# Code placement, SyncE drains and a reshaped last quarter in a fused row-dot and softmax kernel

## The chip, the cores and the metric

One core of a Trainium2 chip. The metric is the device time of one execution in microseconds (us); lower is better. Each run also has its *span*, the time between the first and the last recorded instruction. The timed figure is about 2 us longer than the span.

## The reference

```python
# x, y: 8 x 4096 x 512 fp32
gram = np.matmul(x, y.transpose(0, 2, 1))
diag = np.diagonal(gram, axis1=1, axis2=2)      # 8 x 4096: one dot of 512 per row
diag = diag - diag.max(axis=-1, keepdims=True)
exp = np.exp(diag)
return exp / exp.sum(axis=-1, keepdims=True)
```

Only the diagonal is needed: 32,768 dots of 512 elements, then eight softmaxes of 4096. Both inputs, 134.22 MB, must be read once.

## The kernel before

Four batches lie on 128 partitions (32 partitions each), so two halves of four steps make S = 8 steps. One step is 32 rows for each partition. Helpers used below: `products` is one wide multiply on VectorE, in place in x; `sums` is one reduction on VectorE; `sums_act` is one ScalarE copy per row with an accumulator; `dots` is one fused multiply-and-sum per row on VectorE; `largest` is a maximum over columns on VectorE. K = 6: `side` is ScalarE's copy of the last six rows of y, so that y's only buffer comes free before they are multiplied. The columns of `diag` beyond C = 128 hold maxima.

```python
xs = [big.tile([P, R, D], f32, name=f"xs{i}") for i in range(2)]   # R = 32, D = 512
ys = big.tile([P, R, D], f32, name="ys")                           # one buffer only
diag = [small.tile([P, C + 2 * i], f32, name=f"diag{i}") for i in range(B // Q)]  # C = 128
# ... helpers cut ...
for t in range(S - 2):                       # steps 0 to 5
    load_x(t, 0, R)
    load_y(t, 0, R)
    nc.scalar.activation(out=side, in_=ys[:, R - K :, :], func=Act.Copy)
    products(t, 0, R - K, ys[:, : R - K, :])
    # ... (finish half 0 during step 4) ...
    products(t, R - K, K, side)
    sums(t, 0, R - W)
    sums_act(t, R - W, W)                    # W = 2 rows on ScalarE
    # ... (maximum and exponential of half 0 at the end of step 3) ...

t = S - 2                                    # step 6
load_x(t, 0, R)
for r0 in (0, H):                            # H = 16
    load_y(t, r0, H)
    dots(t, r0, H)

t += 1                                       # step 7, in ever smaller pieces
r0 = 0
for n in (16, 8, 4, 2, 1, 1):
    load_x(t, r0, n)
    load_y(t, r0, n)
    if r0 == 0:
        largest(diag[1][:, C : C + 1], diag[1][:, : C - R])
    if r0 == R - 2:
        largest(diag[1][:, C + 1 :], diag[1][:, C - R : C - 2])
    dots(t, r0, n)
    r0 += n

for p in range(0, P, G):                     # store half 0
    nc.sync.dma_start(out=ov[0, p : p + G, :], in_=res[0][p : p + G, :])
normalize(1, exps(1, diag[1][:, C - 2 :]))   # max, exp, sum, scale
nc.scalar.dma_start(out=ov[1], in_=res[1])   # store half 1
```

## Time and profile before

| | before |
|---|---|
| timed, median of 3 (range) | 321.22 us (321.2 to 321.28) |
| span of the profiled run (timed 321.27) | 319.15 us |
| first load issued / first packet / last load landed | 0.73 / 1.76 / 314.15 us |
| VectorE busy | 76% |

In the profile's timeline a line gives start, duration, engine, line of the program and operation, `output<-input`, and in brackets the idle time before it with what ended it. "SPq" and "ACTq" are DMA issues. The trace also records each DMA packet and each of the 16 increments by which a load tells that its 16 parts have landed (512 increments for the 27 loads and 5 stores of the kernel before). "Spread" below is the time from a load's first increment to its last. Here are the start and the end of the timeline of the kernel before:

```profile
0.73 1.28 ACT L116 ACT_TABLE_LOAD   x1 [0.73 <-PEq L162]
0.73 0.39 SPq L63 DMA_DIRECT2D xs<-in_x_dram  x1
...
312.97 0.18 DVE L97 TENSOR_REDUCE diag<-diag 128x1 f32<-128x30 f32 x1
313.08 0.68 DVE L83 SCALAR_TENSOR_TENSOR xs<-xs,ys 128x512 f32<-128x512 f32 x1
...
314.24 0.69 DVE L83 SCALAR_TENSOR_TENSOR xs<-xs,ys 128x512 f32<-128x512 f32 x1 [0.48 <-DMA ys<-in_y_dram]
...
315.17 0.21 DVE L91 TRANSPOSE_TENSOR_REDUCE nmx<-mxp 128x1 f32<-128x32 f32 x1
315.48 0.40 ACT L104 ACTIVATE res<-diag,nmx 128x128 f32<-128x128 f32 x1 [61.06 <-DVE nmx L91]
...
316.77 0.37 ACTq L147 DMA_DIRECT2D out_dram<-res  x1
```

The reader should see that the very last dot waits for data (0.48 us), and that what follows it is a short serial chain: maximum over partitions (`nmx`), exponential, scaling, and ScalarE's store of half 1.

### The profile page before, as it was taken

The page shows a single profiled execution, that of the slowest core. Times are in us where ns is not written, and L with a number is a line of the kernel's source. Part 1 is how long each engine was busy: PE and PEld are TensorE (multiplying, and loading weights), DVE is VectorE, ACT ScalarE, POOL GpSimd, SP SyncE. Part 2 cuts the span into 40 slices and gives each one's busy share as a digit, 9 for nine tenths or more (in the row PEclk, how much of TensorE's full clock was granted, in tenths as well). Part 3 has the DMA queues.
Part 4 walks back from the last instruction along what each step waited for, and adds up shares of the span by engine and source line. Part 5 has one row for each costly group of instructions (what it writes and reads, how often), then busy time and mean ns, then how long its engine had stood idle before and what let it go on. Part 6 is the DMA issues. An engine that isn't in the chain of part 4 may idle for free.

```text
span 319.2 us, 318 instructions
## 1 busy us (share of the span) xinstructions
DVE 242.8 (76%) x158; ACT 26.9 (8%) x35; POOL 0.2 (0%) x4
## 2 busy tenths in 40 slices
DVE  0000079994899939999399994999949999993995
ACT  1000030100301003010110103001030100000000
POOL 0000000000000000000000000000000000000000
DMA  9999999999999999999999999999999899999992
GB/s 394 394 394 509 411 394 493 427 394 427 493 394 394 517 402 394 493 427 394 435 485 394 394 517 402 394 493 427 394 427 493 378 411 444 412 452 409 421 410 100
DMA packets 4226, 134.36 MB, mean 421 GB/s; under 512 B 513, under 2 KB 769, under 8 KB 1537
## 3 DMA queue, kind: packets, MB, share of 16 engines
q1 hardware_dynamic: 4080, 134.29, 97.8%
q10 hardware_dynamic: 144, 0.07, 0.1%
q14 instruction: 2, 0.01, 0.0%
HBM read 134.22 MB, written 0.13 MB: 421 GB/s over the span
## 4 chain that ended last, share of the span: by engine, by line
DMA 61%; DVE 36%; issue 2%; SPq 0%; ACT 0%; DVEq 0%; ACTq 0%
DMA ys<-in_y_dram 61%; DVE xs L70 27%; DVE xs L83 5%; DVE diag L73 4%; SPq L63 0%; DVE res L111 0%; ACT res L104 0%; DVE nmx L91 0%; DVE sum L91 0%; DVE rc L110 0%; DVE mxp L97 0%; SPq L66 0%; DVEq L70 0%; DVEq L83 0%; ACTq L104 0%
## 5 line engine op out<-in xcount | busy, mean ns | idle before, releaser
L70 DVE TENSOR_TENSOR xs<-xs,ys 128x13312 f32<-128x13312 f32 x6 | 84.1, 14025 | 67.1 <-DMA ys<-in_y_dram 67.1
L73 DVE TENSOR_REDUCE diag<-xs 128x30 f32<-128x15360 f32 x6 | 96.9, 16153 | 0.2
L83 DVE SCALAR_TENSOR_TENSOR xs<-xs,ys 128x512 f32<-128x512 f32 x64 | 39.7, 686 | 5.5 <-DMA ys<-in_y_dram 5.5
L116 ACT ACTIVATE side<-ys 128x3072 f32<-128x3072 f32 x6 | 16.6, 2764 | 123.6 <-DMA ys<-in_y_dram 123.6
L70 DVE TENSOR_TENSOR xs<-xs,side 128x3072 f32<-128x3072 f32 x6 | 20.1, 3350 | 0.0
L78 ACT ACTIVATE xs<-xs 128x512 f32<-128x512 f32 x12 | 7.5, 621 | 88.2 <-DVE xs L70 88.2
L104 ACT ACTIVATE res<-diag,nmx 128x128 f32<-128x128 f32 x2 | 0.8, 401 | 76.6 <-DVE nmx L91 76.6
L83 DVE DVE_READ_ACCUMULATOR xs<-xs,ys 128x1 f32 x64 | 5.2, 82 | 0.0
L78 ACT ACTIVATION_READ_ACCUMULATOR xs<-xs 128x1 f32 x12 | 2.2, 187 | 0.0
L116 ACT ACT_TABLE_LOAD x1 | 1.3, 1283 | 0.7 <-PEq L162 0.7
L91 DVE TRANSPOSE_TENSOR_REDUCE sum<-sump 128x1 f32<-128x32 f32 x2 | 0.4, 207 | 0.6 <-ACT res L104 0.6
L111 DVE TENSOR_SCALAR res<-res,rc 128x128 f32<-128x128 f32 x2 | 0.6, 286 | 0.1
L97 DVE TENSOR_REDUCE mxp<-diag 128x1 f32<-128x128 f32 (+1 forms) x2 | 0.4, 222 | 0.1
L97 DVE TENSOR_REDUCE diag<-diag 128x1 f32<-128x96 f32 (+1 forms) x2 | 0.4, 218 | 0.1
L91 DVE TRANSPOSE_TENSOR_REDUCE nmx<-mxp 128x1 f32<-128x32 f32 x2 | 0.4, 211 | 0.1
L110 DVE RECIPROCAL rc<-sum 128x1 f32<-128x1 f32 x2 | 0.3, 163 | 0.1
L104 ACT ACTIVATION_READ_ACCUMULATOR res<-diag,nmx 128x1 f32 x2 | 0.4, 187 | 0.0
L162 POOL MEMSET const-uint8-127<- 128x1 uint8 x1 | 0.1, 103 | 0.0
L162 POOL MEMSET const-bfloat16-1.0<- 128x1 bf16 x1 | 0.1, 102 | 0.0
L162 POOL MEMSET const-float32-0.0<- 128x1 f32 x1 | 0.1, 99 | 0.2 <-issue 0.2
L162 POOL MEMSET const-float32-1.0<- 128x1 f32 x1 | 0.1, 99 | 0.0
## 6 DMA issues: line engine op xcount, KB each, us to landing
ys<-in_y_dram SPq DMA_DIRECT2D x3, 4096.0 KB, 15.1
xs<-in_x_dram SPq DMA_DIRECT2D x1, 4096.0 KB, 15.2
xs<-in_x_dram SPq DMA_DIRECT2D x1, 2048.0 KB, 19.7
ys<-in_y_dram SPq DMA_DIRECT2D x1, 2048.0 KB, 20.0
xs<-in_x_dram SPq DMA_DIRECT2D x1, 1024.0 KB, 22.1
ys<-in_y_dram SPq DMA_DIRECT2D x1, 1024.0 KB, 22.6
xs<-in_x_dram SPq DMA_DIRECT2D x1, 512.0 KB, 23.5
ys<-in_y_dram SPq DMA_DIRECT2D x1, 512.0 KB, 23.9
```

The lines of the kernel that those rows point to most:

```text
L70: nc.vector.tensor_tensor(out=xt, in0=xt, in1=yt, op=Alu.mult)
L73: nc.vector.tensor_reduce(out=dots_of(t, r0, n), in_=rows(t, r0, n), axis=X, op=Alu.add)
L78: nc.scalar.activation(out=row, in_=row, func=Act.Copy, accum_out=dots_of(t, r, 1))
L83: nc.vector.scalar_tensor_tensor(out=xt, in0=xt, scalar=1.0, in1=ys[:, r, :], op0=Alu.mult, op1=Alu.mult, accum_out=dots_of(t, r, 1),)
L91: nc.vector.tensor_reduce(out=got, in_=column.to_broadcast([P, G]), axis=X, op=op, negate=negate, apply_transpose=True)
L97: nc.vector.tensor_reduce(out=out, in_=d, axis=X, op=Alu.max)
L104: nc.scalar.activation(out=res[i], in_=diag[i][:, :C], func=Act.Exp, bias=nmx, scale=1.0, accum_out=sump)
L110: nc.vector.reciprocal(out=rc, in_=total)
L111: nc.vector.tensor_single_scalar(out=res[i], in_=res[i], scalar=rc, op=Alu.mult)
L116: nc.scalar.activation(out=side, in_=ys[:, R - K :, :], func=Act.Copy)
L162: nc = _bacc.Bacc("TRN2", target_bir_lowering=False, num_devices=1)
```

## The change

Its intent: keep instruction fetches out of the data stream by aligning the start of VectorE's and ScalarE's code (`addr_align(128)`; a slot below is the place of one instruction in an engine's code, and a fetch is an 8192 B packet of the DMA queue that the profile calls "instruction", q14, taken by that name to bring an engine more of its code); make VectorE's code short by using wide instructions in step 6 and giving 24 of its 32 row sums to ScalarE; and shorten the last waits.

```diff
-    diag = [small.tile([P, C + 2 * i], ...
+    diag = [small.tile([P, C + i], ...
@@ ahead of the first step
+    nc.vector.addr_align(128, offset=0, max_nops=0)
+    nc.scalar.addr_align(128, offset=0, max_nops=0)
+    nc.sync.drain()
+    nc.sync.drain()
@@ step 6
         load_y(t, r0, H)
-        dots(t, r0, H)
+        products(t, r0, H, ys[:, r0 : r0 + H, :])
+    sums(t, R - H // 2, H // 2)
+    sums_act(t, 0, R - H // 2)
@@ step 7
-        load_x(t, r0, n)
+        if r0 < R - 1:
+            load_x(t, r0, max(n, 2))
         load_y(t, r0, n)
-        if r0 == 0:
-            largest(diag[1][:, C : C + 1], diag[1][:, : C - R])
         if r0 == R - 2:
-            largest(diag[1][:, C + 1 :], diag[1][:, C - R : C - 2])
+            largest(diag[1][:, C:], diag[1][:, : C - 2])
@@ end
+    met = small.tile([P, C - R], f32, name="met")
+    nc.scalar.activation(out=met, in_=diag[1][:, : C - R], func=Act.Copy)
-    (store of half 0 in four pieces of 32 partitions)
+    (store of half 0 in pieces of 32, 32, 32, 16, 16 partitions)
```

More of the change, by code (lines that the diff above doesn't have):

```diff
@@ L47 @@
     side = big.tile([P, K, D], f32, name="side")
-    diag = [small.tile([P, C + 2 * i], f32, name=f"diag{i}") for i in range(B // Q)]
+    diag = [small.tile([P, C + i], f32, name=f"diag{i}") for i in range(B // Q)]
     res = [small.tile([P, C], f32, name=f"res{i}") for i in range(B // Q)]
@@ L134 @@
     for n in (16, 8, 4, 2, 1, 1):
-        load_x(t, r0, n)
+        if r0 < R - 1:
+            load_x(t, r0, max(n, 2))
         load_y(t, r0, n)
-        if r0 == 0:
-            largest(diag[1][:, C : C + 1], diag[1][:, : C - R])
         if r0 == R - 2:
-            largest(diag[1][:, C + 1 :], diag[1][:, C - R : C - 2])
+            largest(diag[1][:, C:], diag[1][:, : C - 2])
         dots(t, r0, n)
         r0 += n
-    for p in range(0, P, G):
-        nc.sync.dma_start(out=ov[0, p : p + G, :], in_=res[0][p : p + G, :])
+    met = small.tile([P, C - R], f32, name="met")
+    nc.scalar.activation(out=met, in_=diag[1][:, : C - R], func=Act.Copy)
+    for p, n in ((0, G), (G, G), (2 * G, G), (3 * G, G // 2), (3 * G + G // 2, G // 2)):
+        nc.sync.dma_start(out=ov[0, p : p + n, :], in_=res[0][p : p + n, :])
     normalize(1, exps(1, diag[1][:, C - 2 :]))
```

## The prediction

> **What bounds the kernel now.** I read the page's header and DMA rows first, then the DMA queues, the chain of waits in order of time, the waits of the DMA-issuing engine (SyncE), the timeline of the last steps, and last the single packet records and semaphore increments in the trace.
>
> ```profile
> DMA  9999999999999999999999999999999899999992
> ...
> HBM read 134.22 MB, written 0.13 MB: 421 GB/s over the span
> ```
>
> The 16 DMA engines are busy in every slice but the last. By the packet records the first load packet starts at 1.76 us and the last ends at 313.68 us: 134.22 MB in 311.92 us, 430 GB/s, and in between the queue never runs dry. So the time is a head of 1.8 us, a full stream of 311.9 us, a tail from the last landing (314.15 us) to the span's end (319.15 us), and some 2.1 us that the timed 321.22 us has over the span. Work on VectorE or ScalarE matters only if it starves the stream or lies in the tail.
>
> ```profile
> L70 DVE TENSOR_TENSOR xs<-xs,ys 128x13312 f32<-128x13312 f32 x6 | 84.1, 14025 | 67.1 <-DMA ys<-in_y_dram 67.1
> L73 DVE TENSOR_REDUCE diag<-xs 128x30 f32<-128x15360 f32 x6 | 96.9, 16153 | 0.2
> L83 DVE SCALAR_TENSOR_TENSOR xs<-xs,ys 128x512 f32<-128x512 f32 x64 | 39.7, 686 | 5.5 <-DMA ys<-in_y_dram 5.5
> ```
>
> VectorE is busy 76% and waits for data: 67.1 us ahead of the wide products, 5.5 us ahead of the row dots. The last wait column says that data comes late, not work.
>
> The chain of waits, in order of time, at its end:
>
> ```profile
> 269.14 14.79 DVE xs L83 x48
> ...
> 283.95 20.04 DMA ys<-in_y_dram
> ...
> 304.05 10.10 DMA ys<-in_y_dram
> ...
> 314.24 0.71 DVE xs L83 x2
> ...
> 314.98 0.17 DVE mxp L97
> ...
> 315.17 0.22 DVE nmx L91
> ...
> 315.48 0.07 ACT res L104
> ...
> 316.45 0.29 DVE res L111
> ```
>
> It goes through step 6's dots (269.14 on), since they free the y buffer for step 7. But the load released at 283.95 needs 20.04 us to land because it stands behind others in a full queue; that dependency has slack. Only from 314.24 on is everything serial: the last row's dot, maximum, exponential, sum, scaling and store.
>
> One more line, from the DMA view of 274 to 276 us:
>
> ```profile
> q14 instruction: 1, 0.01, 1.0%
> ```
>
> This is an instruction fetch in the middle of the stream, the only 8 KB one inside the span: by its record it starts at 274.53 us, takes 324 ns and moves 8192 B. VectorE alone is working then, in the ninth dot of step 6. The engine that carried it started its next 32 KB packet 308 ns late, and that packet took 1875 ns instead of about 1215. So this engine lost 0.31 + 0.66 = 0.97 us. A load counts as landed when the last of 16 engines has reported. Before 274 us the 16 increments of a load lie within 0.75 to 0.80 us; from the load that lands at 284.47 us on within 0.97 to 1.09 us, with one engine alone at the end. For the last load the increments stand at ..., +523, +702, +1014 ns: the last row waits 0.31 us for that engine alone.
>
> [...]
>
> **The change part by part.**
>
> (1) Aligned code. VectorE's program in the kernel before is 110 instructions, of which 64 dots also read an accumulator: 174 slots. Row nine of step 6 is slot 48[...]. The change takes out 32 dots (64 slots) and adds two products and a sum, so about 113 slots[...]. ScalarE goes from about 50 slots to about 100 (24 more row sums of two slots each)[...]. The fetch moves to the entry, about 0.7 us, ahead of the first data packet at 1.76 us, and both engines have 40 us to spare there (VectorE idle until 42.25). Worth: 1014 - 702 = 0.31 us on the last landing. I take no more, since the second slowest engine then sets it.
>
> (2) Two drains of SyncE ahead of the first load. At the end of the trace two SyncE drains start at 318.421 and 318.479: 58 ns apart. Two cost 0.12 us, and all of it is on the path, since the stream starts that much later. Perhaps they let the moved fetches go first.
>
> (3) Step 6 as products of 16 rows and sums. The first product ends near 269.14 + 8.69 = 277.8, so y's first half is freed 1.2 us earlier than the load at 279.05; the second near 286.4, so y(7) rows 16 to 23, issued at 283.95 before, go out 2.5 us later. Neither matters: the x half-load issued at 269.26 keeps the engines fed until 284.5, and the next until 299.2. Slack is over 6 us and over 12 us. The sum of 8 rows costs 16,153 x 4096/15360, about 4.4 us, so VectorE is done near 290.8, against the 294.2 at which it is next fed. ScalarE: 24 rows at 0.63 us (59.58 to 60.21) are 15.1 us, from 277.9 to about 293; the first reader is the maximum at about 312.9. Worth: nothing on the path.
>
> (4) x of the last two rows in one load. Median packets are 87 ns for 2 KB and 160 ns for 4 KB: 8 x (2 x 87 - 160) = 0.11 us less per engine; I take 0.10. The last y row still ends the stream. The last dot no longer needs two waits. In the trace the last landing (314.151) leads to a separate semaphore instruction at 314.178 and the dot at 314.243; without it the dot follows some 30 ns behind the landing, 0.06 us saved. On the other side the previous y row now lands only one row load (0.66 us) ahead of the end; its dot takes 0.61, so it just fits. The maximum over 126 columns instead of 30 costs 0.28 instead of 0.18 us, in front of that dot, where 0.48 us were idle.
>
> (5) The extra copy on ScalarE runs near 293, with 22 us to spare. It makes ScalarE wait early for its own column sums, which the exponential waited for through a separate semaphore instruction (315.414, exponential at 315.477): 0.06 us saved in the tail. Five output stores of the first half instead of four still hang on the load at 311.53; the last is done well before the final store (318.34).
>
> Sum: -0.31 + 0.12 - 0.10 - 0.06 - 0.06 = -0.41 us, so 320.81 us, if all works. I lean a little toward trouble: 320.85.
>
> **The rivals.**
>
> A. The fetch doesn't leave the stream, or the branch to the aligned code makes fetches that fall after 1.9 us and hold up an engine at the start instead. For: a fetch in the stream cost its engine 0.97 us, and there are 1.1 us between entry and the first packet; two engines now branch. Against: the drains give it 0.12 us more. Then the 0.31 us are not gained: about 321.1; on one of the slow engines up to 0.97 us later, 321.8.
>
> B. SyncE's own program, two slots longer, crosses a block near 311 us and fetches in the last stores, with no time to hide it: 321.2 to 321.7.[...] Against: no such fetch is in the trace before.
>
> C. The later release of y starves the stream, or ScalarE's row sums hold the maximum. The slack of (3), 12 and 19 us, speaks against both; a gap would show at once as an idle DMA slice and cost 1 to 3 us.
>
> D. The last two dots become the bound, since y of row 30 comes late: VectorE would add up to 0.1 us, 320.9.
>
> **Range and chances.** The largest gain that I can name is 0.53 us without the drains, 320.7; a bit more if the stream's order helps. A and B in their common forms reach 321.2 to 321.4. I give the main path 60%, D 10%, A and B 25%, C and the unforeseen 5%. So 320.85 us, with 320.4 to 321.4 holding it 8 times in 10. Faster by over 2% means 314.8, hardly more than the last landing, impossible by this account: 0.01. Slower by 2% is 327.6, which needs a real starvation: 0.01. Within 2%: 0.98.
>
> **What would show it.** Step 1: no instruction packet between 2 and 313 us, and the last load's increments within about 0.75 us. Step 2: the first load issued at about 0.85 instead of 0.73. Step 3: products of 128x8192 at 8.69 us, row sums on ScalarE done near 293, DMA busy throughout. Step 4: no idle time over 0.1 us before the last dot, which starts near 313.9. Step 5: no semaphore instruction just before the last exponential. An instruction packet still in the stream, or a DMA gap around 284 to 300, would make the prediction wrong.

-0.31 for the fetch, +0.12 for the drains, -0.10 for the packets, -0.06 for the last dot and -0.06 for the exponential come to -0.41 us, 320.81, leaned to 320.85. That the alignment moves the fetch to the entry stands in step 1 as an assumption. A "block", here and in the expectations, is the code from one fetch to the next; that a fetch moves with the code, and how far two stood apart, is measured under `vector16`. The 8.69 us of step 3: two products in the trace of the kernel before give the same estimate; 14,025 ns for 13,312 columns and 3,350 for 3,072 make, on a straight line, 8,688 ns for 8,192. That a load counts by its last engine is seen at the last row: its last dot starts at 314.243 us, 0.09 us behind the last of the 16 increments and 0.40 us behind the one before it.

## The result, and the profile after

| | before | after |
|---|---|---|
| timed, median of 6 (range) | 321.25 us (321.14 to 321.56) | 320.73 us (320.56 to 320.94) |
| ratio, 95% interval | | 0.9983 (0.997 to 0.9996) |
| spans | 319.15 (profiled run) | 318.8 to 319.2, profiled run 319.16 |
| timed minus span | 2.12 (profiled run) | 1.78 (profiled run) |

A ratio is the mean time of one kernel's runs over that of the other's of the same rounds, so not quite the ratio of the medians. The change is worth 0.5 us, 0.2%: "within 2%", inside the range of the prediction and close to its 320.85. But the profiled run of the changed kernel is the slowest of its six (320.94), and its span, 319.16 us, is as long as that of the kernel before. In this pair of traces the whole difference of 0.33 us lies *outside* the span (2.12 against 1.78 us). So the time was right, and the prediction's account of it needs checking.

The DMA row and traffic of the changed kernel, then its groups of instructions by shape:

```profile
DMA  9999999999999999999999999999999899999993
...
HBM read 134.22 MB, written 0.13 MB: 421 GB/s over the span
```

```profile
L83 DVE SCALAR_TENSOR_TENSOR xs<-xs,ys 128x512 f32<-128x512 f32 x32 | 20.0, 686 | 3.2 <-DMA ys<-in_y_dram 3.2
L70 DVE TENSOR_TENSOR xs<-xs,ys 128x8192 f32<-128x8192 f32 x2 | 17.3, 8681 | 0.0
...
L73 DVE TENSOR_REDUCE diag<-xs 128x8 f32<-128x4096 f32 x1 | 4.4, 4420 | 0.0
```

The stream is as full as before. Step 6 costs VectorE what was predicted: 8,681 ns for a product (8,690 predicted; the line through two products of the kernel before, given above, makes 8,688) and 4,420 ns for the sum.

The DMA view around the place where the kernel before had its instruction fetch (274 to 276 us), and then that of the stream's start (1.5 to 4 us), both of the changed kernel:

```profile
DMA packets 30, 0.82 MB, mean 410 GB/s; under 512 B 5, under 2 KB 5, under 8 KB 5
## 3 DMA queue, kind: packets, MB, share of 16 engines
q1 hardware_dynamic: 30, 0.82, 95.2%
```

```profile
q1 hardware_dynamic: 16, 1.05, 118.4%
q14 instruction: 2, 0.02, 3.1%
```

The instruction queue, q14, is gone from the middle; two 8 KB packets now stand at the head. By their records they start at 1.97 us (lasting 925 ns) and at 2.83 us (307 ns), while the first load packet starts at 1.87. They are among the data, not ahead of it. The start and the end of the timeline:

```profile
0.83 0.39 SPq L63 DMA_DIRECT2D xs<-in_x_dram  x1
1.15 1.28 ACT L123 ACT_TABLE_LOAD   x1 [1.15 <-PEq L173]
...
313.23 0.28 DVE L97 TENSOR_REDUCE diag<-diag 128x1 f32<-128x126 f32 x1
313.66 0.69 DVE L83 SCALAR_TENSOR_TENSOR xs<-xs,ys 128x512 f32<-128x512 f32 x1 [0.15 <-DMA ys<-in_y_dram]
...
314.31 0.69 DVE L83 SCALAR_TENSOR_TENSOR xs<-xs,ys 128x512 f32<-128x512 f32 x1
...
315.48 0.40 ACT L104 ACTIVATE res<-diag,nmx 128x128 f32<-128x128 f32 x1 [21.97 <-DVE nmx L91]
```

The first load is issued 0.10 us later and the last dot starts 0.06 us later than before, now without an idle time of its own. The exponential starts at the same 315.48.

### The profile page after: what moved, and what is told of

It reads as the page before. It is cut to its first block, busy times and chain, and to the rows that moved or that the text cites. A ratio compares the mean times of both kernels' runs of the same rounds, so it can differ in the third digit from the quotient of the medians.

```text
span 319.2 us, 305 instructions
## 1 busy us (share of the span) xinstructions
DVE 244.7 (77%) x96; ACT 42.0 (13%) x84; POOL 0.2 (0%) x4
## 4 chain that ended last, share of the span: by engine, by line
DMA 62%; DVE 35%; issue 2%; SPq 0%; ACT 0%; DVEq 0%
DMA ys<-in_y_dram 62%; DVE xs L70 30%; DVE diag L73 4%; DVE xs L83 0%; SPq L63 0%; DVE res L111 0%; DVE sum L91 0%; DVE nmx L91 0%; ACT res L104 0%; DVE rc L110 0%; DVE mxp L97 0%; DVEq L70 0%; SPq L66 0%; SPq L118 0%; SPq L117 0%
## 5 line engine op out<-in xcount | busy, mean ns | idle before, releaser
L70 DVE TENSOR_TENSOR xs<-xs,ys 128x13312 f32<-128x13312 f32 (+1 forms) x8 | 101.4, 12689 | 67.6 <-DMA ys<-in_y_dram 67.6
L73 DVE TENSOR_REDUCE diag<-xs 128x30 f32<-128x15360 f32 (+1 forms) x7 | 101.3, 14477 | 0.2
L78 ACT ACTIVATE xs<-xs 128x512 f32<-128x512 f32 x36 | 22.2, 616 | 111.7 <-DVE xs L70 111.7
L83 DVE SCALAR_TENSOR_TENSOR xs<-xs,ys 128x512 f32<-128x512 f32 x32 | 20.0, 686 | 3.2 <-DMA ys<-in_y_dram 3.2
L78 ACT ACTIVATION_READ_ACCUMULATOR xs<-xs 128x1 f32 x36 | 6.7, 186 | 0.0
L83 DVE DVE_READ_ACCUMULATOR xs<-xs,ys 128x1 f32 x32 | 2.6, 81 | 0.0
```

Source lines behind the costliest of these rows:

```text
L70: nc.vector.tensor_tensor(out=xt, in0=xt, in1=yt, op=Alu.mult)
L73: nc.vector.tensor_reduce(out=dots_of(t, r0, n), in_=rows(t, r0, n), axis=X, op=Alu.add)
L78: nc.scalar.activation(out=row, in_=row, func=Act.Copy, accum_out=dots_of(t, r, 1))
L83: nc.vector.scalar_tensor_tensor(out=xt, in0=xt, scalar=1.0, in1=ys[:, r, :], op0=Alu.mult, op1=Alu.mult, accum_out=dots_of(t, r, 1),)
```

## The experiments

Two theories went into them. **P**, the prediction's: the fetch leaves the stream, so the last landing comes 0.3 us earlier. **Q**, the rival from the first pair of traces: the fetch is only moved to the stream's start and costs the same there, and the gain lies in the tail's waits and outside the span. Twelve experiments ran, all correct (two of them repeat the changed kernel), each with five timed runs beside nine of the kernel before on the same chip. All twelve were "same" at the 2% level, so differences are read from ranges, means and traces. The first four shared one chip, the next four a second, the last four a third.

The numbers of all of them; spans are to 0.1 us, and a mean span is the mean of such figures. "First packet" and the fetches inside the span (8 KB packets of the instruction queue) are of the one profiled run, as is "spread", of the last row's load.

| kernel | median us | mean span | timed minus span | first packet | fetches at | spread |
|---|---|---|---|---|---|---|
| before (first trace) | 321.22 | | 2.12 | 1.76 | 274.53 | 1.01 |
| after (first trace) | 320.73 | 318.97 | 1.77 | 1.87 | 1.97, 2.83 | 1.01 |
| *chip one:* before | 321.30 | 319.19 | 2.13 | | | |
| again | 320.53 | 318.74 | 1.79 | 1.86 | 1.76, 1.96 | 0.81 |
| no_drains | 320.75 | 319.00 | 1.78 | 1.75 | 1.77, 4.99 | 0.82 |
| no_align | 320.87 | 319.16 | 1.80 | 1.85 | 260.37, 298.34 | 1.23 |
| drains8 | 320.87 | 319.10 | 1.77 | 2.16 | 1.77, 1.89 | 0.74 |
| *chip two:* before | 321.17 | 319.11 | 2.13 | | | |
| align_only | 321.87 | 320.12 | 1.78 | 1.75 | 1.75, 4.96, 298.69 | 2.12 |
| drains_only | 321.43 | 319.36 | 2.13 | 1.84 | 273.43 | 1.17 |
| step6_only | 320.86 | 319.18 | 1.79 | 1.74 | 258.77, 298.79 | 1.13 |
| tail_only | 320.84 | 318.98 | 1.96 | 1.76 | 273.56 | 1.14 |
| *chip three:* before | 321.30 | 319.21 | 2.12 | | | |
| vector16 | 321.37 | 319.30 | 2.14 | 1.73 | 269.12, 316.17 | 1.17 |
| scalar16 | 321.77 | 320.02 | 1.77 | 1.74 | 274.39, 316.57 | 1.02 |
| drains4 | 320.97 | 319.16 | 1.79 | 1.96 | 1.76, 1.90 | 0.60 |
| again2 | 320.72 | 318.90 | 1.80 | 1.85 | 1.75, 1.92 | 0.79 |

**again: the changed kernel once more.** No edit.

> The changed kernel once more, to see how far its traces differ. In its first trace both fetched blocks fell into the first microsecond of the stream (1.97 and 2.83 us) and the last load's increments still lay 1.01 us apart. Theory P (the prediction: the fetch leaves the stream, the last landing comes 0.3 us earlier): a trace with the fetches ahead of the first packet and a spread near 0.75 us, span about 318.8. Theory Q (the fetch is only moved to the start of the stream and costs the same there; the gain lies in the tail's waits and outside the span): spread near 1.0 us again, span 318.8 to 319.2, and a difference of timed us minus span of about 1.75 against 2.05 in the kernel before. Time 320.7 under both.

Measured: 320.53 us (320.48 to 320.59), ratio 0.9976 (0.9963 to 0.9988). The first fetch starts 0.1 us ahead of the first packet, the spread is 0.81 us instead of 1.01, and the last landing is at 313.85. Here is the end of its timeline:

```profile
312.74 0.28 DVE L97 TENSOR_REDUCE diag<-diag 128x1 f32<-128x126 f32 x1
313.20 0.69 DVE L83 SCALAR_TENSOR_TENSOR xs<-xs,ys 128x512 f32<-128x512 f32 x1 [0.17 <-DMA ys<-in_y_dram]
...
313.87 0.69 DVE L83 SCALAR_TENSOR_TENSOR xs<-xs,ys 128x512 f32<-128x512 f32 x1
...
315.04 0.40 ACT L104 ACTIVATE res<-diag,nmx 128x128 f32<-128x128 f32 x1 [22.01 <-DVE nmx L91]
```

The last dot starts at 313.87 instead of 314.24, and the exponential at 315.04 instead of 315.48. So P is right in this run, and Q in the first trace. In neither are both fetches ahead of the data: here the second starts 0.10 us behind the first packet, in the first trace 0.96 us behind it. What the runs show on this is gathered below, under step 1. What Q said of the time outside the span holds in both (1.79 against 2.13).

**no_drains: the changed kernel without the drains.**

```diff
-    nc.sync.drain()
-    nc.sync.drain()
```

> The changed kernel without the two drains of SyncE. P, with the drains as a pure delay of 0.12 us: 320.6. If the drains exist to let the fetches go ahead of the first packets, the fetches now land behind even more of the first packets and the time is the same or up to 0.3 us longer, 320.7 to 321.0. Q: the fetches are in the stream either way, so 0.12 us shorter, 320.6, first load issued at 0.72 us.

Measured: 320.75 us (320.66 to 320.90), slower than `again` on the same chip, and the two ranges don't touch. The first load is issued at 0.73, 0.10 us earlier, yet the last landing is at 314.24. One fetch starts together with the first packets (1.77 us, lasting 718 ns; 324 in the stream of the kernel before) and the other comes at 4.99, when the first load packets of 64 KB have just ended. The expectation that the drains are a pure delay failed. In the presence of the alignment they are worth about 0.2 us on this chip; that they work by letting the fetches go earlier fits with the traces (step 1 below).

**drains8: eight drains instead of two.**

```diff
-    nc.sync.drain()        (twice)
+    nc.sync.drain()        (eight times)
```

> The changed kernel with eight drains instead of two, so that the first load is issued some 0.35 us later (about 1.18 us) and the first packet starts at about 2.2 us, behind a fetch that starts at 1.97. P: at least one fetch is out of the stream; if both are, the spread of the last load falls to about 0.75 us and 0.3 us comes back, time 320.7 to 320.8. Q (fetches in the head cost nothing that could be won back): 0.35 us longer, 321.05.

Measured: 320.87 us (320.74 to 320.99). The first load is issued at 1.14 us, both fetches are over by 2.27, and the spread falls to 0.74 us, what the kernel before had until its fetch. From first packet to last landing the stream takes 312.06 us here, against 312.39 in the first trace of before, 312.42 in the first trace of after and 311.99 in `again`. So the stream is 0.33 to 0.40 us shorter where both fetches come at its very start, with the share of the x pair's larger packets in it. The six extra drains cost 0.31 us at the start and give back nothing that `again` did not have.

**no_align: the changed kernel without the alignments.**

```diff
-    nc.vector.addr_align(128, offset=0, max_nops=0)
-    nc.scalar.addr_align(128, offset=0, max_nops=0)
```

> The changed kernel without the two alignments. Both theories: VectorE crosses a block near its 50th slot, now the eighth dot or so of step 7 (about 299 us), and ScalarE crosses one in step 6's row sums (about 278 to 293 us), so two fetches are in the last 40 us of the stream. P: the last landing is at least 0.3 us later than with a fetch ahead of the stream, time 321.0 to 321.3. Q: a fetch costs its engine about 1 us wherever it is, so the spread at the end stays near 1.0 and the span does not change, while us minus span goes back to 2.05 if the alignment is what changed it: 321.0.

Measured: 320.87 us (320.83 to 321.29). The two fetches are back in the stream, at 260.37 and 298.34 us, and the spread goes from 0.96 us ahead of the first one to 1.26 and more behind it; the second adds nothing to the last landing: it brings another DMA engine to 1.26 us, level with the slowest. The expectation had the first of the two at 278 to 293 us, in step 6's row sums; why it comes at 260 was not found. The time outside the span stays at 1.80, so the alignment is not the only thing that brings that down. Against `again` the alignment is worth 0.3 us by the medians, all of it in the span.

**align_only: the alignment alone, on the kernel before.**

```diff
+    nc.vector.addr_align(128, offset=0, max_nops=0)
+    nc.scalar.addr_align(128, offset=0, max_nops=0)
```

> The kernel before with VectorE's and ScalarE's code aligned and nothing else. [...] P: no gain from the stream, since a fetch remains in it; 321.2. Q: if the alignment shortens what lies outside the span, us minus span falls from 2.05 to 1.75 and the time is 320.95 although the stream is not better.

Measured: 321.87 us, 0.7 us *slower* than before, ratio 1.002 (1.0006 to 1.0033), although the time outside the span fell to 1.78 as Q said. VectorE's code is still 174 slots long, and a fetch is in the stream in step 7, at 298.69 us (DMA view, 298 to 300 us):

```profile
q1 hardware_dynamic: 59, 0.87, 103.7%
q14 instruction: 1, 0.01, 1.0%
```

The spread was 1.2 us from the start on, by the fetches at the entry, and goes to 2.2 us behind this one; the last increment of the last row stands 1.38 us behind the one before it. The step of about 1 us is the same 0.97 us that the fetch cost its engine in the kernel before. The two fell on the same DMA engine: before this fetch one engine alone stands behind the others (at 1.21 us, the next at 0.77), and behind it again one alone (at 2.20, the next at 0.76); another engine would have made a second straggler. The expectation of no loss was wrong: here the alignment was a loss on code of 174 slots, with which a fetch stayed in the stream; with the 113 or so of the changed kernel none did.

**drains_only: two drains, nothing else.**

```diff
+    nc.sync.drain()
+    nc.sync.drain()
```

> The kernel before with two drains on SyncE and nothing else. As a pure delay: first load issued at 0.84 instead of 0.73 us, time 0.12 us longer, 321.37, us minus span unchanged. If the two slots instead shift SyncE's own code so that its end or the epilogue gets cheaper, us minus span falls to about 1.75 and the time is 321.05.

Measured: 321.43 us (321.26 to 321.80), ratio 1.0007 (0.9995 to 1.002), no clear difference. The first load is issued at 0.83 us, 0.10 later, close to the 0.12 expected. The mean is 0.25 us longer; with this scatter the size beyond the 0.10 is not settled. Outside the span nothing changes (2.13), so SyncE's two slots are not the cause there.

**step6_only: step 6 alone.**

```diff
-        dots(t, r0, H)
+        products(t, r0, H, ys[:, r0 : r0 + H, :])
+    sums(t, R - H // 2, H // 2)
+    sums_act(t, 0, R - H // 2)
```

> The kernel before with step 6 as two products and sums on both engines, nothing else. Step 3 of the prediction: products of 128x8192 at 8.69 us, sums on ScalarE done near 293, no idle DMA slice, nothing gained or lost on the path; fetches: VectorE's moves to about 299 us, ScalarE may add one near 285. P: 321.2 to 321.3. Q: if the smaller number of VectorE slots shortens what follows the span, us minus span falls to 1.75 and the time to 320.95.

Measured: 320.86 us (320.83 to 321.38), span 319.18 against 319.11: nothing gained on the path, as the prediction said of this part, with its two fetches at 258.77 and 298.79. But the time outside the span is 1.79 instead of 2.13. This part is worth 0.3 us in a place where the prediction did not look.

**tail_only: the tail's part alone** (the x pair, one maximum, the copy, five stores; the diff above from step 7 on).

> The kernel before with the tail's part alone: x of the last two rows in one load, one maximum over 126 columns, the copy on ScalarE, five stores. Steps 4 and 5 of the prediction: 0.10 us from the packets, 0.06 from the last dot's second wait, 0.06 from the exponential's: 321.0. The first trace of the changed kernel speaks against part of it: its last dot started 0.02 us behind the landing but 0.64 us behind the dot before, which had begun only at 313.66. If VectorE's pair of dots has become the bound, only the exponential's 0.06 us is left: 321.15. us minus span unchanged at 2.05.

Measured: 320.84 us (320.76 to 321.21). The span is 0.13 us shorter in the mean, less than the scatter of the five (318.8 to 319.3), and the time outside it 0.17 us (1.96). From the start of the maximum over partitions to that of the exponential it takes 0.246 us instead of 0.307; the same two figures, to 2 ns, appear in all the other kernels with and without this part, except one that stalls there on purpose. So the exponential's second wait was worth 0.06 us, as predicted. The last two dots start at 313.68 and 314.30, the second 0.04 us behind its landing and 0.62 us behind the first: in the other kernels with this part it stands 0.02 us behind. So what the expectation feared is worth 0.02 us, in this trace alone.

**vector16 and scalar16: which engine's code costs time outside the span.** Two of the parts, step 6 and the alignment, each bring that time to 1.78, and both change the slots of both engines. So each engine's code was shifted alone, by 16 drains, at a place where the engine has 40 us to spare (in the kernel before the first work on loaded data starts at 42.17 us on ScalarE and at 42.25 on VectorE).

```diff
+    for _ in range(16):
+        nc.vector.drain()      # vector16; nc.scalar.drain() in scalar16
```

> The kernel before with 16 drains at the head of VectorE's program, which shift its code by 16 slots and cost it nothing that counts (it waits there until 42 us). The timed us minus span was 2.13 us in the kernel before and with drains on SyncE, 1.96 with the tail's part (two VectorE slots fewer, one ScalarE slot more), 1.78 with step 6's part or the alignment. Theory V: VectorE's code ends just at a block boundary[...], and the wait for a fetch follows the span; shifted by 16 it goes: us minus span 1.78, time 320.9. Theory S: it is ScalarE's code that ends at a boundary: 2.13 stays, time 321.25. Under both the fetch in the stream comes earlier than 273.4 to 274.5 us, as 16 slots are eight dots: near 269 us.

> The kernel before with 16 drains at the head of ScalarE's program, nothing else. Theory S[...]: us minus span falls to 1.78; the crossing is now inside the kernel, so a second fetch shows in the stream, somewhere between 150 and 260 us, and the span grows by 0 to 0.3: time 320.9 to 321.2. Theory V: us minus span stays 2.13, time 321.25 to 321.5.

Measured: with VectorE shifted, 321.37 us (321.10 to 321.97), outside the span 2.14, no change, and the fetch in the stream went from 274.5 to 269.12 us, 5.4 us earlier and near 269 as computed: this fetch is VectorE's. A second one shows at 316.17 us, in the tail, 139 of VectorE's records further on, and is taken for VectorE's next; it cost nothing that can be seen, since from the maximum to the store's issue it takes 1.79 us as before. With ScalarE shifted, 1.77. So the time outside the span comes from where ScalarE's code lies, as theory S said. That it is a wait for a fetch behind the span is inferred from the stalls below: no trace records a fetch or an instruction there. Nor is it shown why the tail's part, with one more record on ScalarE, takes half of it away (1.96). But the time did not fall, it rose to 321.77 (ratio 1.0015, 1.0002 to 1.0027), for a fetch now stands in the kernel's tail, at 316.57 us, not at 150 to 260 us as expected. Here is the end of the timeline of scalar16:

```profile
315.02 0.21 DVE L91 TRANSPOSE_TENSOR_REDUCE nmx<-mxp 128x1 f32<-128x32 f32 x1
315.63 0.40 ACT L104 ACTIVATE res<-diag,nmx 128x128 f32<-128x128 f32 x1 [61.27 <-DVE nmx L91]
...
316.92 1.16 ACTq L150 DMA_DIRECT2D out_dram<-res  x1
```

The exponential starts 0.61 us after the maximum instead of 0.31, and ScalarE's store takes 1.16 us to issue instead of 0.37: 1.09 us of stalls, with an 8 KB fetch at 316.57 us between them. If the wait behind the span was of the same kind, it costs more ahead of the last store than behind it (1.09 against 0.35 us).

**drains4 and again2: four drains beside two, on one chip.**

```diff
-    nc.sync.drain()        (twice)
+    nc.sync.drain()        (four times)
```

> The changed kernel with four drains instead of two: first load issued at about 0.94 us, first packet near 1.97. With two drains the first fetch started at 1.76 to 1.97 and the second at 1.96 or 2.83 us in two traces, with eight both were done by 2.22 and the increments lay 0.74 us apart. If four let both pass in every run, the collision's up to 0.3 us is saved for 0.1 us of delay: 320.55 to 320.65, no faster than the good runs with two but steadier. If the fetches are rarely in the way with two, 320.65 against 320.55.

> The changed kernel a third time, beside the one with four drains on the same chip. Its runs should fall into 320.5 to 320.9, with spans of 318.7 to 319.2 by where the two fetches fall, and us minus span 1.78. A trace with a span above 319.0 should show a fetch behind the first packets, one at 318.7 none.

Measured: 320.97 us (320.53 to 321.32) with four, 320.72 (320.48 to 321.00) with two. The one trace with four drains is the cleanest of all: fetches over by 2.26 us, spread 0.60, span 318.75. Yet its other runs reached spans of 319.5, and of those there is no trace. So fetches in the head are not all that makes runs differ; what else does stays open. The trace of `vector16`, its slowest run, shows such a thing: between the landings at 42 and 119 us its stream falls 0.6 us behind that of the kernel before, and no fetch is recorded there. Four drains are not better, and no version found beats the changed kernel. What the second expectation said of spans above 319.0 stays untested, for the one trace has a short span. The trace of `again2` (span 318.78) is like that of `again`, a fetch 0.1 us ahead of the first packet and a spread of 0.79.

## Why the prediction was right or wrong

The time and the verdict were right: 320.73 measured, 320.85 predicted, range 320.4 to 321.4. The working was right in most steps inside the span, in runs where the fetches come early enough, and it missed one place altogether. That 320.85 came so close is partly luck: in the first pair of traces nothing of the predicted 0.41 us was gained inside the span, and 0.34 us that the prediction did not have were gained outside it.

- **What bounds the kernel: right.** The stream is full in every trace, and no part moves the time by more than 0.7 us.
- **Step 1, the fetch leaves the stream: right only in part.** In no trace of the changed kernel is a fetch behind 5 us. But there are two at the head of every kernel with the alignment, and in the first trace they were among the data, which is rival A; that trace gains nothing on the stream. In these traces what decides is how late they start. In the three in which a fetch starts 0.9 us or more behind the first packet (`after`, `no_drains`, `align_only`), the first load is complete 21.45 to 21.48 us behind that packet; in the four in which both start at most 0.1 us behind it (`again`, `again2`, `drains4`, `drains8`), 20.96 to 21.09; in the kernel before 21.06. The loads that follow keep what was lost. In `again` the stream from first packet to last landing takes 311.99 us against 312.39, 0.40 us less; the prediction had 0.31 + 0.10 for the fetch and the packets together. The engine whose fetch it was lost 0.97 us, and only 0.3 of it reached the last landing, since before it that engine had been among the first (1.09 - 0.97 = 0.12 us behind the earliest): which engine a fetch falls on matters. Alone, on the long code, the alignment loses 0.7 us.
- **Step 2, the drains as a cost of 0.12 us: the delay is right (0.10 us at the first issue), the sign of the effect wrong beside the alignment.** Against no drains they gain about 0.2 us there, on one chip, and step 1's figures fit the reason that the prediction mentioned as a "perhaps" and gave no number for.
- **Step 3, step 6 is worth nothing on the path: right for the span, wrong for the time.** The product came out within 10 ns. The sum's 4,420 ns fit the prediction's "about 4.4", but its expression, 16,153 x 4096/15360, makes 4.31. ScalarE's sums ended at 293.2 us as computed, and the span did not change; rival C did not show. But the timed figure fell by 0.3 us through what follows the span. It also makes VectorE's code short: aligned, 174 slots had a fetch in the stream at 298.69 us (`align_only`), the 113 or so of the changed kernel none.
- **Step 4: right for the wait, too high for the packets.** The last dot starts 0.02 us behind its landing, against 0.09 in all kernels without this part. From the landing of y's rows 28 and 29 to that of the last row it takes 2.55 to 2.61 us with the x pair and 2.62 to 2.64 without, in the mean 0.04 less (0.07 by the first increments), where 0.10 was expected. Rival D showed in `tail_only` alone, by 0.02 us.
- **Step 5, the exponential: right,** 0.06 us, in every kernel that has this part. Rival B did not show: no trace of the changed kernel has a fetch near 311 us.
- **The sum:** -0.41 us inside the span. By the means of the spans it was -0.45 on chip one and -0.31 on chip three. Outside the span another 0.33 and 0.32 us were gained, a term that the prediction did not have. It had taken "some 2.1 us that the timed 321.22 us has over the span" for fixed, and this is the step that failed. The term comes from where ScalarE's code lies: shown by shifting it alone. That a fetch is waited for behind the kernel's instructions is inferred and was not seen.

From `again` the account of one trace against that of the kernel before closes: first packet +0.10, stream -0.40, landing to dot -0.07, exponential -0.06, in all -0.43 of a span difference of 0.44 us.

## What to carry to other kernels

When the stream of loads is full from end to end (430 GB/s here from the first load packet to the last), look at what else uses the DMA engines: here one 8 KB instruction fetch in the stream cost its engine 0.97 us, and a load was as late as its latest engine (the last row waited 0.31 us for one alone). Placing code helped (0.3 us by the medians, `again` against `no_align`) where no fetch was then left in the stream, and lost 0.7 us where one was (`align_only`). Check where fetches fall for each engine, at the end of the kernel too: where ScalarE's code lay was worth 0.35 us outside the span (1.77 in `scalar16` against 2.12). Parts of such a change don't add up (the alignment alone lost 0.7 us, the drains alone gained nothing), so test them both alone and by taking each out of the whole.

## What else the traces show of fetches, branches and drains

- The large packets of the instruction queue are 8192 B in all these traces (others of it move 32 B or less), and aligning to 128 took the fetches out of the middle of the stream in all six traces of kernels with step 6's short code (none behind 5 us). In `vector16` two fetches, of one packet each, stand 139 records of VectorE apart. No run aligned to another number, so that 128 is the right one is not shown.
- In the kernel before the fetch held up VectorE by nothing that can be seen: its dots around 274.53 us start 0.612 to 0.613 us apart, as the others there do. But the DMA engine that carried the fetch lost 0.97 us for a packet of 0.32 us, and every later load landed about 0.33 us later. For ScalarE at the end of a kernel there were 1.09 us of stalls when a fetch fell ahead of the last store (`scalar16`), and, as far as is inferred, 0.35 us when it fell behind the span.
- In the changed kernel's first trace a branch, which the kernel before does not have, ran at 0.72 us on ScalarE, which went on at 1.15 us, while the fetches started at 1.97 and 2.83 us (1.75 or later in every kernel with the alignment): the branch cost about 0.4 us, and these fetches were not what it waited for. They came 1 us or more behind it, and in that trace fell among the first data.
- At the head, the records of the drains that are there without being asked for take 7 to 10 ns on SyncE, VectorE, ScalarE and TensorE; GpSimd's took 41 and 181 ns, and at the end those just behind the last work took up to 326. An explicit one delays the next instruction by more than its record: 51 to 60 ns start to start on SyncE, 33 on ScalarE (`scalar16`), 40 on VectorE (`vector16`).
